# A forward substitution moved from VectorE to GpSimd in a hybrid decoder step, with the products that use it placed 29 pieces later

## The chip, the cores and the metric

The kernel runs on one NeuronCore of a Trainium2 chip, with five engines that run side by side: TensorE (PE in the profile), VectorE (DVE), ScalarE (ACT), GpSimd (POOL) and SyncE (SP), which here issues the DMA transfers. Each engine takes its instructions in the order in which they stand in its own queue; an instruction that waits for another engine holds up everything behind it on its own. The metric is the device time of one launch in microseconds. Of several runs the median counts.

## The reference

One inference step of a two-layer decoder for a prompt of 256 tokens, with 16 learned tokens ahead of it, and for 8 samples of one token. The sizes are D = 2048, width E = 4096 and 64 heads of 64. Layer 0 is RWKV-7 time mixing:

```python
def rwkv7_step(S, inp):
    r, d, k, v, kk, b = inp
    sa = jnp.einsum('bhij,bhj->bhi', S, kk)
    S = S * d[:, :, None, :] - sa[..., None] * b[:, :, None, :] + v[..., None] * k[:, :, None, :]
    return S, jnp.einsum('bhij,bhj->bhi', S, r)
...
    rkvz = jnp.einsum('btpd,pde->btpe', xm[:, :, :4], w_rkvz)
...
    S_fin, y = lax.scan(rwkv7_step, S0.astype(f32), ...)
    mean = jnp.mean(y, axis=-1, keepdims=True)
    var = jnp.mean(jnp.square(y - mean), axis=-1, keepdims=True)
    y = (y - mean) * lax.rsqrt(var + GN_EPS) * gn_g + gn_b
    y = y + jnp.sum(r_h * k_h * r_k, axis=-1, keepdims=True) * v_h
    y = y.reshape(B, T, WIDTH).astype(dt) * jax.nn.silu(z)
    return y @ w_out, S_fin.astype(S0.dtype), xn[:, -1]
```

Layer 1 is sliding-window attention. All is in float32. The change is in layer 0, in how the scan over the prompt's 272 tokens is computed.

## The kernel before

**Products.** Every weight matrix is read in tiles of 128 x 512 and split in two halves that TensorE multiplies fast: ACT casts the high half (`whi`, L195), DVE subtracts it from the tile to get the low half (`wlo`, L197), and PE makes three products for each pair (L218 to L220). High and low halves have five buffers each, so DVE can be at most five ahead of PE, and less while ACT waits for a buffer. A **piece** is six such products; a half serves two pieces.

**The mixing stage.** From about 130 to 1276 us PE works through the projections r, k, v, z and the first part of the output projection, piece by piece (`products`, L709). Between pieces it does the work of the scan. `drive` (L610) merges the streams: each stream is a Python generator, and `yield 5` means that its next part stands five pieces later in PE's order. So PE's order is written by hand. DVE, ACT and POOL have no written order: a scheduler places each of their instructions in its engine's queue when the program is built, and the queue is fixed from then on.

**The scan in chunks.** The tokens are taken in chunks of 64. Within a chunk the recurrence becomes a triangular system, which needs the inverse of a unit triangular 64 x 64 matrix for each head and chunk. Two units (four heads) are treated together; there are eight such **windows**, o = 0 to 7. In each:

- `scores` (L984) makes the matrices on PE, and ends with two sets of transposes of the keys (L1049, `ps_bk`).
- `substitute` (L1053) inverts the 16 x 16 diagonal blocks. POOL masks the blocks into N (L1064 to L1067), DVE transposes them to NL so that rows lie along the free dimension (L1069), and then come 14 steps, each a product into a scratch tile (L1075) and a sum into NL (L1077) that needs it, with 28 to 112 elements a partition. Two fills set the diagonal (L1079). DVE transposes the result twice, to TN (L1081) and TR (L1082), and ACT spreads TR into TT (L1085).
- `solve` (L1089) makes the 64 x 64 inverse of the blocks with small products on PE, the first of which read TN (L1102, `ps_so`). They stand 24 pieces (27 from o = 5 on) behind the last key transposes.
- `chain` (L1155) carries the state through the five chunks with this inverse.
- `group_norm` (L1256) normalises the window's result, turns it on PE in four turns (L1275, `ps_yt`) and evacuates each with one DVE instruction (L1276). Turns one and two share one pair of PSUM banks, turns three and four the next pair, and the pool has one pair: the third turn waits for the first two evacuations. These turns stand 36 pieces behind their chain, which is within the next window's substitution.

`prep` (L858) prepares the next units meanwhile. Six of its small copies for the samples (L932, `sm`) are on POOL.

Of the kernel before, what the change touches and what calls it, by code (L numbers as in the profile page):

```python
# [109 lines left out]
class Kernel:  # L110
# [942 lines left out]
    def substitute(self, o):  # L1053

        nc, rp = self.nc, self.rp
        V, A, G = nc.vector, nc.scalar, nc.gpsimd
        MU, AD = ALU.mult, ALU.add
        ND, N16, Noff = self.ND, self.N16, self.Noff
        w = lambda n, *s: rp.tile([128, *s], F32, tag=n, name=f"{n}{o}")
        ev = lambda n, *s: rp.tile([128, 512], F32, tag="ev", bufs=2, name=f"{n}{o}")[:, :s[0] * s[1]].rearrange(  # L1060
            "p (i t) -> p i t", t=s[1])
        mask = lambda i, n: self.cst(C_M16 + 16 * i, 16).unsqueeze(1).to_broadcast((128, n, 16))
        t1, t2 = ev("nd1", 20, 16), ev("nd2", 20, 16)
        G.tensor_tensor(t1, ND[:, :, 0:16], mask(0, 20), op=MU)  # L1064
        G.tensor_tensor(t2, ND[:, :, 16:32], mask(1, 20), op=MU)
        G.tensor_tensor(N16[:, 0:20], t1, t2, op=AD)
        G.tensor_tensor(Noff[:, :, 16:32], ND[:, 0:16, 16:32], mask(2, 16), op=MU)  # L1067
        NL = w("NL", 512)
        V.transpose(NL, N16.rearrange("p i t -> p t i"))  # L1069
        nl = NL.rearrange("p (t a s) -> p t a s", a=2, s=16)  # L1070
        for s in range(1, 15):
            n = 15 - s
            tmp = rp.tile([128, 112], F32, tag="stmp", name=f"stmp{o}_{s}")
            tv = tmp[:, :n * 2 * s].rearrange("p (t a j) -> p t a j", a=2, j=s)
            V.tensor_tensor(tv, nl[:, s + 1:16, :, s:s + 1].to_broadcast((128, n, 2, s)),  # L1075
                            nl[:, s:s + 1, :, 0:s].to_broadcast((128, n, 2, s)), op=MU)
            V.tensor_tensor(nl[:, s + 1:16, :, 0:s], nl[:, s + 1:16, :, 0:s], tv, op=AD)  # L1077
        for a in range(2):
            V.memset(NL[:, 16 * a:512:33], 1.0)  # L1079
        TN, TR = w("TN", 16, 32), w("TR", 16, 32)  # L1080
        V.transpose(TN.rearrange("p s i -> p (s i)"), nl.rearrange("p t a s -> p s a t"))  # L1081
        V.transpose(TR.rearrange("p t i -> p (t i)"), NL)  # L1082
        TT = rp.tile([128, 20, 64], F32, tag="TT", name=f"TT{o}")
        for b in range(4):
            A.activation(TT[:, :, 16 * b:16 * b + 16], TR[:, :, 0:20].rearrange("p t i -> p i t"), AF.Copy,  # L1085
                         scale=self.cst(C_M64 + 16 * b, 1))
        self.TT, self.TN, self.TR = TT, TN, TR

    def solve(self, o):  # L1089

        nc, rp = self.nc, self.rp
        V, A, G = nc.vector, nc.scalar, nc.gpsimd
        Noff, TT, TN, TR = self.Noff, self.TT, self.TN, self.TR
        ev = lambda n, *s: rp.tile([128, 512], F32, tag="ev", bufs=2, name=f"{n}{o}")[:, :s[0] * s[1]].rearrange(
            "p (i t) -> p i t", t=s[1])

        yield 24 if o < 5 else 27
        ps = self.bank(self.pe, f"ps_so{o}")
        Q = [slice(32 * q, 32 * q + 32) for q in range(4)]
        for i in range(16):  # L1100
            for q in Q:
                nc.tensor.matmul(ps[q, 16 * i:16 * i + 16], Noff[q, i], TN[q, :, i], start=True, stop=True)  # L1102
        ET = ev("ET", 16, 16)
        V.tensor_copy(ET, ps[:, 0:256].rearrange("p (i s) -> p i s", s=16))
        yield 4
        for i in range(16):
            for q in range(4):
                nc.tensor.matmul(ps[32 * q:32 * q + 16, 256 + 16 * i:272 + 16 * i], ET[Q[q], i], TR[Q[q], :, i],
                                 start=True, stop=True)
        for q in range(4):  # L1110
            r, c = slice(32 * q, 32 * q + 16), 16 + 32 * (q % 2)
            (A.copy if q % 2 else V.tensor_copy)(TT[r, 0:16, c:c + 16],
                                                 ps[r, 256:512].rearrange("p (i t) -> p i t", t=16))
        TN2 = ev("TN2", 16, 32)
        V.transpose(TN2.rearrange("p i s -> p (i s)"), TT[:, 0:16, 0:32])
        yield 7
        ps = self.bank(self.pe, f"ps_so2{o}").rearrange("p (i s) -> p i s", s=32)
        for i in range(16):
            for q in range(2):
                nc.tensor.matmul(ps[Q[2 * q + 1], i], self.N12[Q[2 * q], i], TN2[Q[2 * q], i], start=True, stop=True)  # L1120
        ET = ev("ET2", 16, 32)
        for q in range(2):
            r = Q[2 * q + 1]
            (A.copy if q else V.tensor_copy)(ET[r], ps[r])
        yield 5
        for i in range(16):
            for q in range(2):
                r = Q[2 * q + 1]
                nc.tensor.matmul(ps[Q[2 * q], i], ET[r, i], TT[r, i, 32:64], start=True, stop=True)
        for q in range(2):  # L1130
            r = Q[2 * q]
            (A.copy if q else V.tensor_copy)(TT[r, 0:16, 32:64], ps[r])
# [840 lines left out]
```

## Time and profile before

| what | value |
|---|---|
| median of 3 runs | 2118.64 us (2115.4 to 2123.16) |
| the profiled execution | 2118.32 us |
| its span, first to last instruction | 2116.5 us |
| TensorE's granted clock | 0.990 of full speed |
| PE busy | 2064.9 us, 98% |
| DVE busy | 1697.8 us, 80%, 4112 instructions |
| ACT busy | 1263.8 us, 60% |
| POOL busy | 122.5 us, 6%, 188 instructions |

A row of a group of instructions names line, engine, operation, the tile written and the tiles read, the shapes, how often, the busy time in us and the mean of one in ns, and then the idle time of the engine just before them and what ended it. A row of the order of time begins with the start and the duration in us. A row of the waits names who waited for whom, us in total, times and the longest. Products of PE overlap, so their starts tell the rate, not their durations.

### The profile page before, as it was taken

The page shows a single profiled execution, that of the slowest core. Times are in us where ns is not written, and L with a number is a line of the kernel's source. Part 1 is how long each engine was busy: PE and PEld are TensorE (multiplying, and loading weights), DVE is VectorE, ACT ScalarE, POOL GpSimd, SP SyncE. Part 2 cuts the span into 40 slices and gives each one's busy share as a digit, 9 for nine tenths or more (in the row PEclk, how much of TensorE's full clock was granted, in tenths as well). Part 3 has the DMA queues.
Part 4 walks back from the last instruction along what each step waited for, and adds up shares of the span by engine and source line. Part 5 has one row for each costly group of instructions (what it writes and reads, how often), then busy time and mean ns, then how long its engine had stood idle before and what let it go on. Part 6 is the DMA issues. An engine that isn't in the chain of part 4 may idle for free.

```text
span 2116.5 us, 55871 instructions
## 1 busy us (share of the span) xinstructions
PE 2064.9 (98%) x21420; PEld 1965.8 (93%) x21420; DVE 1697.8 (80%) x4112; ACT 1263.8 (60%) x2790; POOL 122.5 (6%) x188
## 2 busy tenths in 40 slices
PE   9999999899999999999999999999999999999997
PEld 7999899889899989899999999999999999999997
DVE  8867777687678878888888788997888888878885
ACT  3457766576766757767676445565565655544443
POOL 0011100001010010100100001100000000000000
PEclk9999999999999999999999999999999999999999
DMA  7898667658756876777657687757455444567774
GB/s 258 314 312 250 189 213 241 188 181 290 216 180 205 260 229 198 211 217 222 203 152 246 207 257 243 247 172 227 132 167 156 146 155 130 181 210 247 232 219 132
DMA packets 276356, 446.28 MB, mean 211 GB/s; under 512 B 54056, under 2 KB 97768, under 8 KB 275696
## 3 DMA queue, kind: packets, MB, share of 16 engines
q1 hardware_dynamic: 275656, 441.66, 66.6%
q8 instruction: 168, 2.75, 0.5%
q10 hardware_dynamic: 432, 1.05, 0.1%
q14 instruction: 100, 0.82, 0.1%
HBM read 381.69 MB, written 65.03 MB: 211 GB/s over the span
## 4 chain that ended last, share of the span: by engine, by line
PE 87%; DVE 5%; ACT 3%; DMA 3%; issue 2%; SPq 0%; POOL 0%; DVEq 0%; POOLq 0%; ACTq 0%
PE ps_z L218 6%; PE ps_z L219 6%; PE ps_z L220 6%; PE ps_k L218 3%; PE ps_ob L218 3%; PE ps_ob L220 3%; PE ps_v L218 3%; PE ps_ob L219 3%; PE ps_r L218 3%; PE ps_q L218 3%; PE ps_q L220 3%; PE ps_q L219 3%; PE ps_k L219 3%; PE ps_k L220 3%; PE ps_v L220 3%; PE ps_v L219 3%
## 5 line engine op out<-in xcount | busy, mean ns | idle before, releaser
L218 PE MATMUL ps_z<-mhlm,whi_z 128*128 128x280 f32 x512 | 158.6, 310 | 2.8 <-ACT sr L937 2.0
L219 PE MATMUL ps_z<-mhlm,whi_z 128*128 128x280 f32 x512 | 150.6, 294 | 0.0
L220 PE MATMUL ps_z<-mhlm,wlo_z 128*128 128x280 f32 x512 | 150.3, 294 | 0.0
L218 PE MATMUL ps_q<-bmh,whi_qb 128*128 128x264 f32 x512 | 150.0, 293 | 0.1
L218 PE MATMUL ps_z<-bmh,whi_zb 128*128 128x264 f32 x512 | 147.4, 288 | 0.0
L220 PE MATMUL ps_q<-bmh,wlo_qb 128*128 128x264 f32 x512 | 145.6, 284 | 0.6 <-DVE wlo_qb L197 0.6
L219 PE MATMUL ps_q<-bml,whi_qb 128*128 128x264 f32 x512 | 145.6, 284 | 0.0
L219 PE MATMUL ps_z<-bml,whi_zb 128*128 128x264 f32 x512 | 145.5, 284 | 0.0
L220 PE MATMUL ps_z<-bmh,wlo_zb 128*128 128x264 f32 x512 | 145.4, 284 | 0.0
L218 PE MATMUL ps_ob<-ghi,whi_ob 128*128 128x264 f32 x512 | 145.3, 285 | 0.0
L220 PE MATMUL ps_ob<-ghi,wlo_ob 128*128 128x264 f32 x512 | 144.6, 284 | 0.0
L219 PE MATMUL ps_ob<-glo,whi_ob 128*128 128x264 f32 x512 | 144.6, 283 | 0.0
L195 ACT CAST whi_ob<-raw_ob 128x512 fp32r<-128x512 f32 x128 | 79.1, 620 | 96.9 <-PE ps_ob L219 77.8
L195 ACT CAST whi_oa<-raw_oa 128x512 fp32r<-128x512 f32 x128 | 79.2, 620 | 88.0 <-PE ps_oa L219 30.6
L197 DVE TENSOR_TENSOR wlo_r<-raw_r,whi_r 128x512 fp32r<-128x512 f32 x128 | 87.8, 691 | 42.6 <-ACT whi_r L195 41.3
L218 PE MATMUL ps_v<-mhlm,whi_v 128*128 128x280 f32 x384 | 119.8, 312 | 0.4 <-ACT st L790 0.4
L218 PE MATMUL ps_k<-mhlm,whi_k 128*128 128x280 f32 x384 | 119.1, 310 | 1.0 <-ACT st L790 1.0
L195 ACT CAST whi_v<-raw_v 128x512 fp32r<-128x512 f32 x128 | 79.0, 619 | 65.8 <-PE ps_v L219 37.7
L197 DVE TENSOR_TENSOR wlo_v<-raw_v,whi_v 128x512 fp32r<-128x512 f32 x128 | 87.3, 687 | 36.9 <-ACT whi_v L195 35.6
L195 ACT CAST whi_zb<-raw_zb 128x512 fp32r<-128x512 f32 x128 | 78.2, 619 | 62.9 <-PE ps_z L219 38.5
L220 PE MATMUL ps_k<-mhlm,wlo_k 128*128 128x280 f32 x384 | 112.4, 293 | 2.1 <-issue 2.1
L219 PE MATMUL ps_v<-mhlm,whi_v 128*128 128x280 f32 x384 | 112.7, 293 | 0.0
(478 smaller groups left out, 7604.1 us busy)
## 6 DMA issues: line engine op xcount, KB each, us to landing
raw_k<-a_w_rkvz SPq DMA_DIRECT2D x128, 256.0 KB
raw_v<-a_w_rkvz SPq DMA_DIRECT2D x128, 256.0 KB
raw_r<-a_w_rkvz SPq DMA_DIRECT2D x128, 256.0 KB
raw_z<-a_w_rkvz SPq DMA_DIRECT2D x128, 256.0 KB
raw_oa<-a_w_out SPq DMA_DIRECT2D x128, 256.0 KB
raw_qb<-b_w_qz SPq DMA_DIRECT2D x128, 256.0 KB
raw_zb<-b_w_qz SPq DMA_DIRECT2D x128, 256.0 KB
raw_ob<-b_w_o SPq DMA_DIRECT2D x128, 256.0 KB
```

The costliest lines, as they stand in the source:

```text
L195: self.nc.scalar.copy(hi, src)
L197: return self.nc.vector.tensor_tensor(lo, src, hi.bitcast(F32), op=ALU.subtract)
L218: mm(ps, wh, xh, start=start, stop=False)
L219: mm(ps, wh, xl, start=False, stop=False)
L220: return mm(ps, wl, xh, start=False, stop=stop)
```

## The change

The 14 steps of the substitution and the two fills of the diagonal are issued on GpSimd instead of VectorE, in all eight windows. The three transposes stay on VectorE. The solve's first products stand 29 pieces behind the last key transposes in every window, instead of 24 (windows 0 to 4) and 27 (windows 5 to 7). Nothing is computed differently.

```diff
@@ substitute @@
         for s in range(1, 15):
             n = 15 - s
             tmp = rp.tile([128, 112], F32, tag="stmp", name=f"stmp{o}_{s}")
             tv = tmp[:, :n * 2 * s].rearrange("p (t a j) -> p t a j", a=2, j=s)
-            V.tensor_tensor(tv, nl[:, s + 1:16, :, s:s + 1].to_broadcast((128, n, 2, s)),
+            G.tensor_tensor(tv, nl[:, s + 1:16, :, s:s + 1].to_broadcast((128, n, 2, s)),
                             nl[:, s:s + 1, :, 0:s].to_broadcast((128, n, 2, s)), op=MU)
-            V.tensor_tensor(nl[:, s + 1:16, :, 0:s], nl[:, s + 1:16, :, 0:s], tv, op=AD)
+            G.tensor_tensor(nl[:, s + 1:16, :, 0:s], nl[:, s + 1:16, :, 0:s], tv, op=AD)
         for a in range(2):
-            V.memset(NL[:, 16 * a:512:33], 1.0)
+            G.memset(NL[:, 16 * a:512:33], 1.0)
@@ solve @@
-        yield 24 if o < 5 else 27
+        yield 29
         ps = self.bank(self.pe, f"ps_so{o}")
```

The scheduler places DVE's and POOL's instructions anew. In window 3 the stretch of DVE's queue around TN and TR reads, before:

```order
L197 TENSOR_TENSOR wlo_r_4_9909<-raw_r_4_9906,whi_r_4_9908 128x512
L1077 TENSOR_TENSOR NL_9548<-NL_9548,stmp_13_9586 128x4x13
L1276 SCALAR_TENSOR_TENSOR vT_5616<-ps_yt_0_9866,par,vT_5616 128x272
L1075 TENSOR_TENSOR stmp_14_9589<-NL_9548 128x28
L1077 TENSOR_TENSOR NL_9548<-NL_9548,stmp_14_9589 128x2x14
L197 TENSOR_TENSOR wlo_r_6_9915<-raw_r_6_9912,whi_r_6_9914 128x512
L1081 STREAM_TRANSPOSE TN_9594<-NL_9548 128x512
L1082 STREAM_TRANSPOSE TR_9595<-NL_9548 128x512
L1276 SCALAR_TENSOR_TENSOR vT_5616<-ps_yt_0_9866,par,vT_5616 128x272
L197 TENSOR_TENSOR wlo_r_8_9950<-raw_r_8_9947,whi_r_8_9949 128x512
L1276 SCALAR_TENSOR_TENSOR vT_6617<-ps_yt_2_9936,par,vT_6617 128x272
```

and with the change:

```order
L197 TENSOR_TENSOR wlo_r_4_9899<-raw_r_4_9896,whi_r_4_9898 128x512
L197 TENSOR_TENSOR wlo_r_6_9905<-raw_r_6_9902,whi_r_6_9904 128x512
L197 TENSOR_TENSOR wlo_r_8_9940<-raw_r_8_9937,whi_r_8_9939 128x512
L1081 STREAM_TRANSPOSE TN_9648<-NL_9602 128x512
L1082 STREAM_TRANSPOSE TR_9649<-NL_9602 128x512
L197 TENSOR_TENSOR wlo_r_10_9963<-raw_r_10_9960,whi_r_10_9962 128x512
L1276 SCALAR_TENSOR_TENSOR vT_5607<-ps_yt_0_9926,par,vT_5607 128x272
L197 TENSOR_TENSOR wlo_r_12_9981<-raw_r_12_9978,whi_r_12_9980 128x512
L1276 SCALAR_TENSOR_TENSOR vT_5607<-ps_yt_0_9926,par,vT_5607 128x272
L197 TENSOR_TENSOR wlo_r_14_10004<-raw_r_14_10001,whi_r_14_10003 128x512
L197 TENSOR_TENSOR wlo_r_0_10027<-raw_r_0_10024,whi_r_0_10026 128x512
L1276 SCALAR_TENSOR_TENSOR vT_6607<-ps_yt_2_9990,par,vT_6607 128x272
```

The steps of the substitution are gone from between the low halves, and both of the first two evacuations (L1276, `vT` from `ps_yt_0`) now stand behind TN, where one stood ahead of it. Between NL's transpose and TN this queue now has one product (L906) and eight low halves.

POOL's queue in the same window, from the masks on, with the change; before, the copies `sm` of L932 followed the masks directly:

```order
L1066 TENSOR_TENSOR N_1741<-nd_9596,nd_9597 128x320
L932 COPY sm_10038<-kT_9684 128x2x8
L1075 TENSOR_TENSOR stmp_1_9604<-NL_9602 128x28
L1077 TENSOR_TENSOR NL_9602<-NL_9602,stmp_1_9604 128x28
L932 COPY sm_10038<-ta_9422 128x2x8
L1075 TENSOR_TENSOR stmp_2_9607<-NL_9602 128x52
L1077 TENSOR_TENSOR NL_9602<-NL_9602,stmp_2_9607 128x26x2
```

The remaining steps follow one another without anything between them but the two fills. In windows 1 and 2 further `sm` copies stand among the steps.

PE's queue in window 3 around the solve's first products, before:

```order
L220 MATMUL ps_r_1_9905<-mhlm_23_2_8572,wlo_r_4_9909 128x280
L1102 MATMUL ps_so_9965<-TN_9594,Noff 32x16 x64
L1275 MATMUL ps_yt_2_9936<-consts,Y 128x128 x3
L218 MATMUL ps_r_0_9904<-mhlm_23_3_8634,whi_r_6_9914 128x280
L219 MATMUL ps_r_0_9904<-mhlm_23_3_8634,whi_r_6_9914 128x280
```

and with the change:

```order
L219 MATMUL ps_r_0_10073<-mhlm_23_0_8404,whi_r_0_10026 128x280
L220 MATMUL ps_r_0_10073<-mhlm_23_0_8404,wlo_r_0_10027 128x280
L1102 MATMUL ps_so_10093<-TN_9648,Noff 32x16 x64
L218 MATMUL ps_r_1_10074<-mhlm_23_0_8404,whi_r_0_10026 128x280
L219 MATMUL ps_r_1_10074<-mhlm_23_0_8404,whi_r_0_10026 128x280
```

Before, they stood between the third and the fourth turn of the group norm (L1275); now they stand five pieces behind the fourth.

## The prediction, made before the change was timed

> **What bounds the kernel now.** I read the page's busy shares first, then the waits of TensorE (PE), then the groups of VectorE (DVE) by line, then GpSimd's (POOL) prices, and last the order of time in two of the eight windows.
>
> From the page, share of the span:
>
> ```profile
> PE 2064.9 (98%) x21420; PEld 1965.8 (93%) x21420; DVE 1697.8 (80%) x4112; ACT 1263.8 (60%) x2790; POOL 122.5 (6%) x188
> ```
>
> PE is busy for 98% of the span and its order is written by hand, so the time changes only by what PE waits for. DVE at 80% is no bound by itself; POOL is nearly idle. PE's waits (us in total, times, longest) that name DVE inside the mixing stage:
>
> ```profile
> PE ps_yt L1275 <- DVE vT L1276: 8.0, 2, 6.9
> PE ps_so L1102 <- DVE TN L1081: 6.1, 2, 3.5
> ...
> PE ps_bo L954 <- DVE vT L955: 1.5, 2, 1.3
> ...
> PE ps_ch L1191 <- DVE X L1227: 1.1, 1, 1.1
> ```
>
> The second row is the substitution being late for the solve's first products: 6.1 us, in two windows of eight. The other six have room. So the most that the edit can win directly is 6.1 us, and all that DVE makes PE wait here is 16.7 us.
>
> **What is taken off DVE.** The groups of DVE by line, from 160 to 1260 us:
>
> ```profile
> L1077 DVE TENSOR_TENSOR NL<-NL,stmp 128x28 f32<-128x28 f32 (+6 forms) x112 | 26.9, 240 | 1.8
> ...
> L1075 DVE TENSOR_TENSOR stmp<-NL 128x28 f32<-128x28 f32 (+6 forms) x112 | 26.6, 238 | 1.6
> ```
>
> 224 small operations, 53.5 us in eight windows: 6.7 us of DVE work in each. DVE isn't the bound, so this is worth what PE waits for it, not 53.5 us.
>
> **What POOL needs for the same.** POOL's two-input operations by line, ns min/median/max:
>
> ```profile
> L1067 POOL TENSOR_TENSOR Noff<-F,consts x8: 737/747/3049, 225.7 to 1135.1; 128x256 f32<-128x256 f32 x8
> ...
> L1065 POOL TENSOR_TENSOR nd<-F,consts x8: 863/989/1335, 228.5 to 1137.1; 128x320 f32<-128x320 f32 x8
> ...
> L1450 POOL TENSOR_TENSOR sqacc<-sqacc,sqa x14: 791/1050/1117, 1291.5 to 1376.0; 128x280 f32<-128x280 f32 x14
> ```
>
> By the fastest of each, 256 elements take 737 ns and 320 take 863: 1.97 ns an element and 233 ns fixed (280 elements: 784, the row has 791). The substitution's products have 28, 52, 72, 88, 100, 108, 112 elements and back down to 28, 1120 in all, and the sums as many. So 28 x 0.233 + 2240 x 0.00197 = 10.9 us undisturbed. Every step needs the one before. The gap between dependent POOL operations, and the small copies that the change's order puts between the steps:
>
> ```profile
> 625.49 0.88 POOL L1065 TENSOR_TENSOR nd<-F,consts 128x320 f32<-128x320 f32 x1
> 626.44 1.21 POOL L1066 TENSOR_TENSOR N<-nd,nd 128x320 f32<-128x320 f32 x1
> 628.02 0.65 POOL L932 COPY sm<-kT 128x16 f32<-128x16 f32 x1 [0.37 <-DVE kT L904]
> 628.67 0.20 POOL L932 COPY sm<-ta 128x16 f32<-128x16 f32 x1
> ```
>
> 0.07 us lies between the first two (625.49 + 0.88 to 626.44): 28 x 0.07 = 2.0 us. Two copies at 0.2 us make 0.4. Sum: 13.3 us with nothing in the way.
>
> **Something is in the way.** The same stretch of window o=4 on both engines:
>
> ```profile
> 742.34 3.05 POOL L1067 TENSOR_TENSOR Noff<-F,consts 128x256 f32<-128x256 f32 x1 [5.81 <-ACT F L1023]
> ...
> 746.93 0.86 POOL L1065 TENSOR_TENSOR nd<-F,consts 128x320 f32<-128x320 f32 x1
> ```
>
> ```profile
> 745.41 0.67 DVE L197 TENSOR_TENSOR wlo_k<-raw_k,whi_k 128x512 fp32r<-128x512 f32 x1
> ...
> 747.15 1.20 DVE L197 TENSOR_TENSOR wlo_k<-raw_k,whi_k 128x512 fp32r<-128x512 f32 x1 [0.44 <-ACT whi_k L195]
> ```
>
> A DVE subtract that takes 0.67 us alone takes 1.20 beside a POOL operation; a POOL operation that takes 0.74 alone took 3.05 beside a run of DVE operations. [...] So the work moved to POOL does not run beside DVE's subtracts for nothing. Between the window's two transposes the changed order has eight low halves and one more two-input product on DVE. What one costs POOL is bounded below by nothing (it falls into POOL's gaps) and above by its whole 0.67 us. I take 0.4, between L1065's median and its slowest against its fastest (0.13 and 0.47) and nearer the latter, since POOL now always has a step waiting. 9 x 0.4 = 3.6: **the chain takes 16.9 us**, between 13.3 and 19.3.
>
> **What is behind it.** The order of the change puts DVE's transposes TN and TR in one place, behind eight low halves, and DVE stands at TN until POOL is through; before, 28 short operations stood there, each ready when its turn came. Behind TN wait a low half, the evacuation of the turned group norm (L1276), another low half and the second evacuation. PE's third turn (L1275) can't start before those two evacuations, since its two banks are single. How long PE takes to get there, in windows 3 and 4 (NL's transpose, TN, the evacuations; PE's third turn):
>
> ```profile
> 628.53 1.07 DVE L1069 STREAM_TRANSPOSE NL<-N 128x512 f32<-128x512 f32 x1
> ...
> 642.50 1.14 DVE L1081 STREAM_TRANSPOSE TN<-NL 128x512 f32<-128x512 f32 x1
> 643.57 0.67 DVE L1082 STREAM_TRANSPOSE TR<-NL 128x512 f32<-128x512 f32 x1
> 644.16 0.46 DVE L1276 SCALAR_TENSOR_TENSOR vT<-ps_yt,par,vT 128x272 f32<-128x272 f32 x1
> 644.54 0.67 DVE L197 TENSOR_TENSOR wlo_r<-raw_r,whi_r 128x512 fp32r<-128x512 f32 x1
> 645.25 0.50 DVE L1276 SCALAR_TENSOR_TENSOR vT<-ps_yt,par,vT 128x272 f32<-128x272 f32 x1
> ```
>
> ```profile
> 644.46 0.29 PE L219 MATMUL ps_r<-mhlm,whi_r 128*128 128x280 f32 x1
> 644.59 0.29 PE L220 MATMUL ps_r<-mhlm,wlo_r 128*128 128x280 f32 x1
> 644.72 0.50 PE L1275 MATMUL ps_yt<-consts,Y 128*128 128x128 f32 x3
> ```
>
> ```profile
> 749.27 1.08 DVE L1069 STREAM_TRANSPOSE NL<-N 128x512 f32<-128x512 f32 x1 [0.92 <-POOL N L1066]
> ```
>
> ```profile
> 768.40 0.38 PE L1275 MATMUL ps_yt<-consts,Y 128*128 128x128 f32 x2
> ```
>
> From NL's end to that turn PE takes 644.72 - 629.60 = 15.1 us and 768.40 - 750.35 = 18.1 us, 16.6 on average. From TN's start to the end of the second evacuation DVE takes 1.66 (642.50 to 644.16) + 0.71 + 0.38 + 0.71 + 0.50 = 4.0 us. So a chain of up to 12.6 us costs nothing, and one of 16.9 makes **PE wait 4.3 us**. This holds in windows 2, 3, 4, 6 and 7: 21.5 us. It comes earlier than the solve's first products, which the 29 pieces move away; they no longer are what is late.
>
> In windows 0 and 5 no evacuation stands behind TN, and the products' low halves are late instead. A low half serves 12 products 0.13 us apart (644.46, 644.59), 1.54 us. There are five buffers, so DVE is at most four ahead, 6.2 us, less the cast and the subtract that refill one:
>
> ```profile
> L195 ACT CAST whi_v<-raw_v 128x512 fp32r<-128x512 f32 x128 | 79.0, 619 | 65.8 <-PE ps_v L219 37.7
> ```
>
> 6.2 - 0.62 - 0.67 = 4.9 us. DVE gets to TN after some 8 x 1.54 = 12.3 us; with 13 two-input operations the chain is 13.3 + 13 x 0.4 = 18.5, DVE stands 6.2, and the next low half comes 6.2 + 1.7 + 0.7 = 8.6 us after the last, where PE wants it after 4.9 + 1.5 = 6.4: about 2.2. Window 0 has eight more such operations ahead of TN; 3 us each, 6 us. In window 1 DVE waits at the same place for a DMA in both kernels; I put 1 us.
>
> **Twenty-nine pieces.** A piece is six products, 0.77 us. The solve moves by 5 pieces five times and by 2 three times: the chain ends 31 x 0.77 = 24 us later in PE's order. PE does other products meanwhile, which costs nothing as long as there are some. Last window:
>
> ```profile
> 1258.39 0.55 PE L1275 MATMUL ps_yt<-consts,Y 128*128 128x128 f32 x3
> ```
>
> ```profile
> 1265.03 1.31 DVE L197 TENSOR_TENSOR glo<-gy,ghi 128x1120 fp32r<-128x1120 f32 x1
> ```
>
> The last turn's result is ready as an operand 1266.34 - 1258.39 = 8.0 us later. The changed order puts 72 products, 9.2 us, between that turn and the operand's first use. I put 0; without this cover it would be up to 8.
>
> **Sum.** 21.5 + 6 + 1 - 6.1 (the waits at L1102 go) = +22.4. The profiled execution took 2118.32 us, 1.8 more than its span and 0.3 under the median: **2141 us**. With a chain of 13.3 us: 5 x 0.7 - 6.1 = -2.6, 2116. With 19.3: 5 x 6.7 + 2 x 6 + 3 - 6.1 = +42, 2161.
>
> The nearest rows for the per-element price have inner rows of 16 elements or more; the substitution's have 1 to 14, with 64 bytes between them. [...]
>
> **The rivals.** *Short rows are dear.* If an element costs 1.55 times as much there (as L1065's slowest row to its fastest), 4.4 x 0.55 = 2.4 us come on top, the chain is 19.3 and the time 2161. For it: nothing in the trace has such rows. Against: L932's 16 elements take 0.20 us. [...]
>
> *The chain fits.* If DVE's two-input work falls into POOL's gaps, the chain is 13.3 to 14.5 us and PE waits 0.7 to 2 us a window: 2116 to 2124, no change that can be measured (0.5%, 10.6 us, is about what a measurement of this kernel can tell). For it: between L1065's median and its fastest lies only 0.13 us. Against: 3.05 for 0.74.
>
> *Faster.* DVE is rid of 6.7 us just where it is fullest. If the chain stays under 12.6 us everywhere, no wait at TN is passed on, and all 16.7 us that DVE makes PE wait could go: 2102. It decides at 12.6 us, under the 13.3 that POOL needs undisturbed; so only a lower fixed price than 233 ns would do it.
>
> **Chances.** The forecast 0.54, dear short rows 0.15, the chain fits 0.24, faster 0.07. The forecast's own range is 2128 to 2156; the range for 8 in 10 reaches down into the case that fits and up past the dear rows: 2112 to 2166. Faster by over 0.5% (under 2108): 0.07; within: 0.25; slower (over 2129): 0.68.
>
> **What would show it.** PE's wait for L1276 at L1275 grows from 8 us to 20 or more, in six or seven windows, and the wait for TN at L1102 is gone. DVE's waits get a row of TN waiting for POOL's NL, 4 to 7 us in each window. POOL's busy time about doubles, and L197 rows beside it take over 1 us. I am wrong in the price if L1075 and L1077 on POOL average far from 0.39 us plus 0.13 of blocking, and in the mechanism if TN starts late and PE doesn't wait, or if PE waits at L1102 still.

## The result: 2169.6 us, 2.4% slower

The changed kernel takes 2169.6 us (median of 4 runs, 2168.12 to 2171.73) against 2118.36 us in the same session: a ratio of 1.024, 95% interval 1.0221 to 1.0259. The prediction said 2141 us, 2112 to 2166: slower it is, but by 51 us and not by 22.

The page of the changed kernel, busy time by engine:

```profile
PE 2081.4 (96%) x21420; PEld 1977.7 (91%) x21420; DVE 1670.5 (77%) x3872; ACT 1263.7 (58%) x2790; POOL 217.9 (10%) x428
```

The span is 2166.3 us, 49.8 more than before. It splits in two. The time in which PE is not busy (span less busy) went from 51.6 to 84.9 us, **33.3 more**. And PE is busy for 2081.4 us where it was 2064.9, **16.5 more, with the same 21420 products**. The prediction spoke of the first part only.

The waits of the changed kernel (us in total, times, longest):

```profile
ACT TT L1085 <- DVE TR L1082: 40.1, 8, 5.8
DVE TN L1081 <- POOL NL L1077: 36.0, 8, 5.7
PE ps_yt L1275 <- DVE vT L1276: 25.3, 6, 5.4
PE ps_z L218 <- ACT st L790: 7.0, 1, 7.0
PE ps_so L1108 <- issue: 5.5, 4, 2.0
```

DVE stands at TN in all eight windows, 4.5 us on average, and ACT at its copies TT for 5.0 (36.0 and 40.1 us in eight windows): ACT too takes its instructions in order, and behind TT stand its casts and the evacuations of PE's results (L790). PE waits for what stands behind the two. Window 3 on DVE:

```profile
642.90 1.08 DVE L1069 STREAM_TRANSPOSE NL<-N 128x512 f32<-128x512 f32 x1
...
653.15 0.69 DVE L197 TENSOR_TENSOR wlo_r<-raw_r,whi_r 128x512 fp32r<-128x512 f32 x1 [0.65 <-ACT whi_r L195]
659.51 1.04 DVE L1081 STREAM_TRANSPOSE TN<-NL 128x512 f32<-128x512 f32 x1 [5.66 <-POOL NL L1077]
660.47 0.67 DVE L1082 STREAM_TRANSPOSE TR<-NL 128x512 f32<-128x512 f32 x1
661.06 0.65 DVE L197 TENSOR_TENSOR wlo_r<-raw_r,whi_r 128x512 fp32r<-128x512 f32 x1
661.63 0.49 DVE L1276 SCALAR_TENSOR_TENSOR vT<-ps_yt,par,vT 128x272 f32<-128x272 f32 x1
```

The eight low halves are done at 653.84, the chain at 659.5; TN starts at once, and the first evacuation ends at 662.12. PE in the same stretch:

```profile
657.13 0.29 PE L219 MATMUL ps_r<-mhlm,whi_r 128*128 128x280 f32 x1
657.26 0.29 PE L220 MATMUL ps_r<-mhlm,wlo_r 128*128 128x280 f32 x1
662.18 0.90 PE L1275 MATMUL ps_yt<-consts,Y 128*128 128x128 f32 x3 [4.63 <-DVE vT L1276]
662.73 0.58 PE L218 MATMUL ps_r<-mhlm,whi_r 128*128 128x280 f32 x1
663.11 0.43 PE L219 MATMUL ps_r<-mhlm,whi_r 128*128 128x280 f32 x1
663.35 0.43 PE L220 MATMUL ps_r<-mhlm,wlo_r 128*128 128x280 f32 x1
```

Ahead of the wait two products start 0.13 us apart; behind it 0.24 (663.11 to 663.35). Here is where PE's extra busy time lies. The same stretch in windows (length, PE busy, PEld, DVE, ACT, POOL, then PE's granted clock, DMA share, GB/s):

```profile
657.00:660.00 3.00, 0.55 (x5) 0.32 (x3) 0.49 (x1) 0.00 (x0) 2.08 (x9) 1.00 0.01 2
660.00:662.00 2.00, 0.00 (x0) 0.00 (x0) 2.00 (x4) 0.83 (x2) 0.00 (x0) 0.54 0.00 0
662.00:664.00 2.00, 1.82 (x8) 1.82 (x9) 1.22 (x3) 2.00 (x4) 0.00 (x0) 0.50 0.38 136
664.00:667.00 3.00, 3.00 (x15) 3.00 (x14) 1.31 (x2) 1.40 (x3) 0.00 (x0) 0.50 0.72 193
667.00:670.00 3.00, 3.00 (x27) 3.00 (x25) 1.26 (x3) 0.85 (x2) 0.00 (x0) 1.00 0.74 238
```

Some 2.6 us after PE has fallen idle (657.55 to about 660.2) its clock goes to half, and it stays there for 6.8 us, 4.8 us of them behind the wait's end. In three microseconds PE starts 15 products at half clock, and 27 in the next three. Over the mixing stage, before and then with the change:

```profile
160.00:1310.00 1150.00, 1116.23 (x13866) 1051.25 (x13866) 914.83 (x2053) 758.89 (x1671) 87.58 (x139) 0.99 0.70 218
```

```profile
160.00:1360.00 1200.00, 1133.84 (x13867) 1064.77 (x13866) 887.11 (x1813) 758.43 (x1672) 182.95 (x379) 0.97 0.67 209
```

The same 13867 products take 17.6 us more, at a granted clock of 0.97 instead of 0.99. Summed over short windows PE spent 34.1 us at half clock before its last product in the kernel before and 68.3 with the change. At a granted clock of 0.50 half of the added 34.2 us, 17.1, is what such time costs by estimate if PE has work throughout; measured are 16.5.

### The profile page after: what moved, and what is told of

Same layout as the page of the kernel before. It is cut to its first block, busy times and chain, and to the rows that moved or that the text cites. A ratio compares the mean times of both kernels' runs of the same rounds, so it can differ in the third digit from the quotient of the medians.

```text
span 2166.3 us, 55895 instructions
## 1 busy us (share of the span) xinstructions
PE 2081.4 (96%) x21420; PEld 1977.7 (91%) x21420; DVE 1670.5 (77%) x3872; ACT 1263.7 (58%) x2790; POOL 217.9 (10%) x428
## 3 DMA queue, kind: packets, MB, share of 16 engines
q8 instruction: 168, 2.75, 0.5%
## 5 line engine op out<-in xcount | busy, mean ns | idle before, releaser
L195 ACT CAST whi_oa<-raw_oa 128x512 fp32r<-128x512 f32 x128 | 79.2, 621 | 87.8 <-PE ps_o L219 34.2
L218 PE MATMUL ps_v<-mhlm,whi_v 128*128 128x280 f32 x384 | 121.2, 316 | 3.0 <-ACT st L790 2.0
L197 DVE TENSOR_TENSOR wlo_r<-raw_r,whi_r 128x512 fp32r<-128x512 f32 x128 | 89.0, 702 | 41.2 <-ACT whi_r L195 39.4
L197 DVE TENSOR_TENSOR wlo_k<-raw_k,whi_k 128x512 fp32r<-128x512 f32 x112 | 77.9, 701 | 55.3 <-ACT whi_k L195 55.1
L197 DVE TENSOR_TENSOR wlo_v<-raw_v,whi_v 128x512 fp32r<-128x512 f32 x128 | 87.8, 691 | 41.5 <-ACT whi_v L195 39.9
L195 ACT CAST whi_zb<-raw_zb 128x512 fp32r<-128x512 f32 x128 | 78.2, 619 | 62.6 <-PE ps_z L219 38.5
L220 PE MATMUL ps_v<-mhlm,wlo_v 128*128 128x280 f32 x384 | 114.1, 297 | 0.0
```

The source lines that it names most:

```text
L195: self.nc.scalar.copy(hi, src)
L197: return self.nc.vector.tensor_tensor(lo, src, hi.bitcast(F32), op=ALU.subtract)
L218: mm(ps, wh, xh, start=start, stop=False)
L220: return mm(ps, wl, xh, start=False, stop=stop)
```

## The experiments

Three theories. **Theory 1**: DVE and ACT stand in order behind GpSimd's chain, and PE's clock halves after each long wait. **Theory 2**: GpSimd and DVE slow each other down. **Theory 3**: the later solve has a price. All twelve kernels, with the two of the case; "not busy" is the span less PE's busy time, "half clock" is summed as above.

| kernel | median us | ratio to before, 95% interval | PE not busy | PE busy | half clock |
|---|---|---|---|---|---|
| before | 2118.36 | 1 | 51.6 | 2064.9 | 34.1 |
| the change | 2169.60 | 1.0240 (1.0221 to 1.0259) | 84.9 | 2081.4 | 68.3 |
| pieces29 | 2127.49 | 1.0048 (1.0032 to 1.0065) | 59.1 | 2066.7 | 27.3 |
| pool_old | 2151.01 | 1.0162 (1.0144 to 1.0180) | 78.2 | 2076.6 | 54.6 |
| late_tn | 2127.19 | 1.0041 (1.0022 to 1.0060) | 61.6 | 2063.8 | 20.5 |
| busy_turn | 2191.93 | 1.0353 (1.0337 to 1.0368) | 83.1 | 2105.7 | 58.0 |
| busy_second | 2167.10 | 1.0226 (1.0207 to 1.0245) | 67.8 | 2096.7 | 30.7 |
| half_chain | 2153.02 | 1.0154 (1.0135 to 1.0173) | 73.5 | 2079.9 | 54.6 |
| late_old | 2128.25 | 1.0041 (1.0026 to 1.0056) | 59.7 | 2069.2 | 41.0 |
| spread29 | 2124.96 | 1.0024 (1.0012 to 1.0035) | 53.6 | 2069.9 | 37.5 |
| act_late | 2165.34 | 1.0231 (1.0216 to 1.0246) | 89.2 | 2079.4 | 64.9 |
| spread_dve | 2117.68 | 0.9997 (0.9981 to 1.0012) | 47.8 | 2062.5 | 20.5 |
| spread_pool | 2118.95 | 1.0004 (0.9992 to 1.0015) | 51.5 | 2062.2 | 17.1 |
| idle_copy | 2144.92 | 1.0131 (1.0106 to 1.0157) | 71.4 | 2071.3 | 47.8 |

Twelve of these kernels have the same 21420 products (all but the two busy ones). Over them PE's busy time rises with its time at half clock, by 0.39 us for each, with a correlation of 0.97.

The three last columns are those of one profiled execution, whose span can lie some us beside the median (spread_dve: 2110.3, at the lower end of its runs).

### The two halves of the change, one at a time

pieces29 is before with the second edit alone, pool_old the change without it:

```diff
# pieces29: against before
-        yield 24 if o < 5 else 27
+        yield 29
# pool_old: against the changed kernel
-        yield 29
+        yield 24 if o < 5 else 27
```

> Only the 29 pieces; the substitution stays on DVE. Theory 1 (DVE and ACT stand in order behind GpSimd's chain, and PE's clock halves after each long wait): nothing of the loss is in the pieces. The 6.1 us of PE's wait for TN at L1102 go and nothing else changes: 2110 to 2122 us, ratio 0.997 to 1.002. Theory 3 (the solve, 24 us later in PE's order, makes what follows it late; the 16 us of new PE waits at L1191, L218 and L1108 are its price): about 2118 + 16 = 2134 us, ratio 1.008, with these waits in the trace.

> Only the substitution on GpSimd; the pieces stay at 24 and 27. Theory 1: the loss is here: 2162 to 2175 us (after: 2169.6), with about 25 us of PE's wait at L1275 and 60 to 75 us at half clock. Theory 3: without the later solve 16 us less than after, about 2153 us.

Neither theory had it whole: pieces29 lies between their numbers, and pool_old even below theory 3's. The 29 pieces cost 10 us by themselves (0.48%), GpSimd's substitution 34 us (1.62%), and the two together some 7 us more than the sum, hardly more than the three intervals leave open. In pool_old the stand is the one of the change, 37.5 us of DVE at TN and 30.8 of PE at L1275, and PE spends 54.6 us at half clock.

What the 29 pieces cost is on the page of pieces29's waits:

```profile
PE ps_so L1108 <- issue: 10.9, 7, 3.3
PE ps_ch L1191 <- ACT X L1227: 3.8, 3, 2.6
PE ps_yt L1275 <- DVE vT L1276: 2.9, 3, 2.3
...
PE ps_ch L1191 <- DVE X L1227: 2.3, 2, 1.4
```

The waits for TN and for the evacuations are as good as gone, as predicted, and in their place PE stands at the solve's second group of products, for nothing that the profile names. A smaller part is theory 3's: in the chain that follows the solve PE waits 6.1 us at L1191, where before has 1.3. Window 3 on PE:

```profile
658.20 1.27 PE L1102 MATMUL ps_so<-TN,Noff 32*32 32x16 f32 x128
662.85 1.23 PE L1108 MATMUL ps_so<-TR,ET 32*16 32x16 f32 x126
667.33 0.21 PE L1108 MATMUL ps_so<-TR,ET 32*16 32x16 f32 x2 [3.25 <-issue]
```

PE runs 126 of 128 products, stands for 3.25 us and then runs the last two, which need nothing that the 126 did not have. In the list of DMA queues over the whole of before stands a row of instructions, and between 664.5 and 666 us of pieces29 one packet of it:

```profile
q8 instruction: 168, 2.75, 0.5%
```

```profile
q8 instruction: 1, 0.02, 3.9%
```

2.75 MB in 168 packets are 16 KB each, and 2 x 21420 products and weight loads in 168 packets are 255 instructions each: this is PE's own program, fetched in blocks. (With the semaphore instructions PE has 43021 records in before, 256 for each packet.) Each of the solve's two groups is 256 instructions in 1.2 us, a block's worth, where elsewhere in the mixing stage one block lasts about 10 us. The packet lands at 665.8 and PE goes on at 667.3. All fourteen traces bear it out. PE stands 70 times for over 0.3 us without a named cause. Counted along PE's records, 68 of these stands fall on the same place in a block of 256, number 193 or 194, and in each of the 68 a packet of this queue lands 1.2 to 1.8 us before PE goes on.

### Is it the clock?

Unused products ahead of a waiting turn take away PE's idleness and no wait. busy_turn has them ahead of the third turn, busy_second ahead of the second:

```diff
+                self.cur = ps[0] if h < 7 else None        # in `products`
 ...
+            for _ in range(18 if j == 2 and self.cur is not None else 0):   # busy_second: j == 1
+                nc.tensor.matmul(self.cur[:, 384:512], self.ident, self.ident, start=False, stop=False)
             for c in range(3):
                 nc.tensor.transpose(ps[:, 128 * c:128 * c + 128], ...
```

> After, with 18 products of 128 x 128 (some 3.8 us, their results are read by nobody) ahead of the third turn L1275 in every window but window 5: PE works where it waited. Theory 1 (a wait of PE is followed by half clock): PE waits 1 us instead of 4 to 5, the half clock behind these turns (41 of the 68 us) goes, and although no work is removed the kernel is up to 41/2 = 20 us faster: 2150 to 2160 us. Rival (the clock has no part; PE's products are slower for another reason): the products fill the wait and change nothing, 2168 to 2173 us.

2191.9 us. The third turn was the wrong place, which corrected the picture: PE's 25 us at the turns stayed, and of the 30.2 us that the seven groups take 22 were simply added. The turn that waits is the second, for the first evacuation (661.63 + 0.49 against 662.18 in the rows above), though the two have a bank each.

> After, with the 18 unused products of 128 x 128 (4.2 us by their 18 in the last run) now ahead of the second turn L1275, which is the one that waits, in windows 2 to 7 (and once behind the last window). Theory 1 (a wait of PE is followed by half clock): PE's 25 us at L1275 fall to about 8 (window 1 has no products), the half clock behind these turns goes (68 us of half clock before, 35 or less now), and although no work is taken out the time falls by 10 to 17 us: 2152 to 2160 us. Rival (PE's products are slower for another reason, the clock follows it): the products fill the waits, 4 us are lost where nothing waits, 2170 to 2176 us.

2167.1 us: the gain did not come, PE's wait at the turns fell to 16.3 us and not to 8, and still the run tells what it was made for. Its page, and the time of the unused products alone:

```profile
PE 2096.7 (97%) x21672; PEld 1994.0 (92%) x21672; DVE 1670.2 (77%) x3872; ACT 1263.1 (58%) x2790; POOL 217.9 (10%) x428
```

```profile
0.00:2165.00 2165.00, 29.26 (x252) 28.80 (x252) 0.99 0.66 206
```

The unused products take 29.3 us. Without them PE is busy for 2096.7 - 29.3 = 2067.4 us, 14 less than in the change and within 2.5 us of before, and its time at half clock is 30.7 us instead of 68.3. So with the idleness the slow clock goes, and the products run at their old pace. That the time did not fall is arithmetic: 14 us of clock and 17.1 us of idleness were won, and 29.3 us of products paid for them.

Over eight of these traces (before, the change, pieces29, pool_old, late_tn, half_chain, act_late, idle_copy) PE waited 2.4 us or longer 52 times; 48 of these waits have a stretch of half clock beginning within 5.5 us of their start. Of 58 waits between 1.4 and 2.4 us, 26 have one. Over all fourteen traces it is 69 of 79 and 41 of 91. Before PE's last product the stretches last 3.4, 6.8, 10.2 or, once in spread29, 13.7 us. So a wait of 2.4 us sufficed in nearly all cases and one of 1.4 in some (the shortest, with no longer wait near it, is 1.43 us at L1102 in the change).

### Is it the standing or the company?

late_tn leaves GpSimd's chain and the 29 pieces as they are, and puts the two transposes behind four more low halves. `issue_after` queues what is in its block behind the named instruction of the same engine; `los` and `his` hold the low halves and the casts issued so far:

```diff
     def substitute(self, o):
 ...
-        TN, TR = w("TN", 16, 32), w("TR", 16, 32)
-        V.transpose(TN.rearrange("p s i -> p (s i)"), nl.rearrange("p t a s -> p s a t"))
-        V.transpose(TR.rearrange("p t i -> p (t i)"), NL)
-        TT = rp.tile([128, 20, 64], F32, tag="TT", name=f"TT{o}")
-        for b in range(4):
 ...
     def solve(self, o):
 ...
-        yield 29
+        yield 25
+        with self.tc.issue_after(self.los[-1].ins):
+            TN, TR = w("TN", 16, 32), w("TR", 16, 32)
+            V.transpose(TN.rearrange("p s i -> p (s i)"), nl.rearrange("p t a s -> p s a t"))
+            V.transpose(TR.rearrange("p t i -> p (t i)"), NL)
+        with self.tc.issue_after(self.his[-1].ins):
+            TT = rp.tile([128, 20, 64], F32, tag="TT", name=f"TT{o}")
+            for b in range(4):
 ...
+        yield 4
```

> After, with the two transposes TN and TR put on DVE behind four more low halves (12 instead of 8), behind the first turned group norm's two evacuations, and ACT's four copies TT likewise later; GpSimd's chain and the 29 pieces stay. Theory 1: nobody stands behind the chain any more. DVE's 36 us of waiting at TN and ACT's 40 us at TT fall below 8, PE's 25.3 us at L1275 and the 7.0 us in window 5 go, and with them the 17 us of slower clock: 2169.6 - 25.3 - 7.0 - 17 = 2120 us, 2105 to 2125. Theory 2 (GpSimd's work beside DVE's slows DVE, whatever stands where): 2150 us or more.

2127.2 us, above the 2105 to 2125 expected, since the 29 pieces have a price of their own; the time is that of pieces29 to 0.3 us. The waits of late_tn:

```profile
ACT TT L1100 <- DVE TR L1096: 9.8, 8, 2.3
PE ps_so L1114 <- issue: 6.5, 5, 2.5
DVE TN L1095 <- POOL NL L1077: 4.8, 4, 1.6
PE ps_yt L1281 <- DVE vT L1282: 4.0, 3, 2.3
```

DVE's stand falls from 36.0 to 4.8 us and ACT's from 40.1 to 9.8, and 42 us of the kernel's time go with them, although GpSimd does the same work beside DVE (230.7 us busy). Theory 2 as it was put, GpSimd's work slowing DVE, has nothing left in this change. The cost lies in where the scheduler put TN against the chain's end. Contention has a share in that all the same: the chain takes some 3.9 us more in each window beside DVE's operations than by its fastest steps (below), and DVE stands 4.5 us there. No run has this chain without DVE's operations beside it.

act_late frees ACT alone: TN and TR stay, only the four copies TT move as above.

> After, with ACT's four copies TT (L1085) put behind the casts of 25 pieces later, and DVE's TN and TR left where after has them: only ACT is freed from standing. If ACT's standing has its own price (window 5: 7.0 us of PE's wait for ACT's st, and its half clock of 10.2 us): ACT's 40 us of waiting for TR fall below 8, the 7.0 us go and 5 us of clock with them, 2158 us (2154 to 2163). If DVE's standing alone sets the time: 2167 to 2172 us.

2165.3 us, 4 less than the change, and the two intervals overlap. PE's 7.0 us in window 5 are gone, and of its other large waits none: that for the evacuations is 29.4 us, and DVE still stands 35.8 at TN. So freeing ACT alone is worth some 4 us, and nearly all of the 42 needs DVE freed. What ACT's standing would cost with DVE free no run shows.

half_chain asks how the price depends on the chain's length. It leaves out steps 8 to 14:

```diff
-        for s in range(1, 15):
+        for s in range(1, 8):
             n = 15 - s
```

> After, with the steps 8 to 14 of the substitution left out (half the elements, 14 of 28 operations), so that GpSimd's chain is about 8 us instead of 15.9. Theory 1 with the bound of the prediction (a chain of up to about 12 us costs nothing): all of the chain's price goes, what is left is that of the 29 pieces: 2127 us, 2122 to 2131. Rival (each us of the chain costs the same, by contention or in the chain of dependences): half of the price goes, about 2148 us.

2153.0 us: more than half of the price is left, and the bound of 12 us is refuted as such. The waits, and window 3 on DVE:

```profile
DVE TN L1081 <- POOL NL L1079: 29.0, 8, 4.2
```

```profile
642.77 0.76 DVE L197 TENSOR_TENSOR wlo_r<-raw_r,whi_r 128x512 fp32r<-128x512 f32 x1 [0.86 <-ACT whi_r L195]
646.88 1.09 DVE L1081 STREAM_TRANSPOSE TN<-NL 128x512 f32<-128x512 f32 x1 [3.36 <-POOL NL L1079]
```

The chain takes 8 us, and DVE still stands 3.6 us in each window, because TN now stands behind three to five low halves instead of seven or eight. With the chain the scheduler moved TN as well, as if it placed TN where it takes the chain to end, and too soon in both kernels. The rival's number (2148) is nearer, but not for the rival's reason.

idle_copy puts GpSimd's load beside before, unneeded by anybody:

```diff
+        X = ev("X", 2, 256)
+        xl = N16.rearrange("p (t a) s -> p t a s", a=2)
+        for s in range(1, 15):
+            ...
+            G.tensor_tensor(xv, xl[:, s + 1:16, :, s:s + 1]..., xl[:, s:s + 1, :, 0:s]..., op=MU)
+            G.tensor_tensor(xw, xl[:, s + 1:16, :, 0:s], xv, op=AD)
         for s in range(1, 15):
```

> Before (substitution on DVE, 24 and 27 pieces), and beside it GpSimd does 28 operations of the same shapes in each window whose results nobody reads: GpSimd's load of after without anybody waiting for it. Theory 1 (only standing in order costs): DVE's two-input operations lose at most 28 x 0.1 us in each window, off PE's path for the most part: 2114 to 2126 us. Theory 2 (contention of the two engines): the 34 us that pool_old lost come back here, 2140 us or more.

2144.9 us, against theory 1 as I had put it. DVE's two groups of the substitution, and the largest wait of PE:

```profile
L1083 DVE TENSOR_TENSOR stmp<-NL 128x28 f32<-128x28 f32 (+6 forms) x112 | 38.7, 345 | 1.5
L1085 DVE TENSOR_TENSOR NL<-NL,stmp 128x28 f32<-128x28 f32 (+6 forms) x112 | 38.2, 341 | 1.9
```

```profile
PE ps_yt L1283 <- DVE vT L1284: 25.3, 9, 8.5
```

Each short operation of DVE takes 343 ns instead of 239, 2.9 us in each window: the size that I had allowed. What I had wrong is that this is off PE's path. The evacuations stand between these operations, PE's wait for them goes from 8.0 to 25.3 us, and some 26 us are lost. The queues are not what changed: PE and ACT have the order of before, and DVE too, but for two pairs of neighbours among 4112, and nobody waits for the added work. Contention is real, then, where both engines run short two-input operations, as here. In the change DVE has none left there, and its large subtracts hardly suffer: in the mixing stage L197 takes 702 ns on average, against 693 before.

### Can the two edits be had without their price?

> The substitution on GpSimd, TN and TR behind two or three more low halves than in after (10 or 11), and the solve's first products at 24 and 27 pieces as before. If the prices of the two parts are separate, the 10 us of the 29 pieces go too and DVE's 53 us of short operations are gone: 2108 to 2118 us. If TN is then late for L1102 (chain 15.9 + transposes 2.2 + NL 1.1 against 24 x 0.77 = 18.5 us), PE waits up to 1 us in each window: 2118 to 2126 us.

late_old is late_tn with 21 pieces to TN and 24 and 27 to the first products. 2128.3 us: TN is not late for L1102, but at 21 pieces it is early for the chain again, and L1275 waits 12.9 us.

spread29 is pieces29 with `yield 8` for the `yield 4` between the solve's two groups; spread_dve and spread_pool keep 27 and 4 pieces in the last window:

```diff
-        yield 29
+        yield 29 if o < 7 else 27
 ...
-        yield 4
+        yield 8 if o < 7 else 4
         for i in range(16):
```

> Pieces29 (the substitution on DVE, 29 pieces) with the second group of products, L1108, 8 pieces behind the first, L1102, instead of 4. Theory A (PE's instructions come from memory in blocks of 16 KB, 256 instructions; the two groups of 128 products and weight loads 3.4 us apart use them faster than they come, so PE stands inside L1108 for 12.3 us in all): the wait inside L1108 falls below 4 us, 2127 - 8 = 2119 us, 2114 to 2122. Theory B (the solve's end comes too late for what follows): 4 pieces more make it worse, 2127 to 2133 us.

The waits of spread29:

```profile
PE ps_oa L218 <- ACT ghi L195: 4.0, 1, 4.0
PE ps_dy L1337 <- DVE dy L1334: 3.4, 1, 3.4
...
PE ps_so L1108 <- issue: 1.5, 2, 1.2
```

Both theories hold a part. Eight pieces apart, the two groups hardly run out of instructions any more: 10.9 us become 1.5. But the last window, with no next one behind which to hide, ends later, and two new waits of 7.4 us stand there.

> Spread29 (substitution on DVE, 29 pieces, L1108 8 pieces behind L1102), but with 27 and 4 pieces in the last window, whose end stood in the way: there PE waited 7.4 us for the last group norm and ran at half clock for 13.7 us. Theory A (the instruction stream sets the price of the 29 pieces): 2125 - 7.4 - 6.8 = 2111 us, 2107 to 2116, faster than before. Theory B (a later solve costs in every window): 2119 to 2125 us.

> Late_tn (substitution on GpSimd, nobody standing behind it) with the same two changes as spread_dve. Late_tn's 9.1 us of PE's wait in the second group of products go, by theory A: 2127 - 9 = 2118 us, 2111 to 2121. If GpSimd's work beside DVE's has a price of its own, spread_pool is slower than spread_dve by it; theory 1 says by 3 us or less, theory 2 (contention) by 10 or more.

2117.7 and 2119.0 us: the price of the 29 pieces is gone in both, and both take what before takes. The first lies 1.7 us above the range expected of it, the second within its own. The last window still costs spread_dve 5.6 us of PE's waits (3.0 at L1337, 2.6 at L1275) and 10.2 us at half clock. Between the two kernels lies 1.3 us, and their intervals overlap, so with nobody standing behind it GpSimd's substitution neither costs nor gains anything that these runs can tell, though it relieves DVE of 32 us (1703.0 to 1671.2 us busy). No version is measurably faster than the kernel before.

## Why the prediction was right and wrong, step by step

- **The waits at L1102 go (6.1 us).** Right: 1.4 us are left, and not for TN.
- **GpSimd's chain takes 16.9 us, 13.3 to 19.3.** Right: 15.9 us on average from first to last step, 15.0 to 17.3. The groups of the changed kernel:

```profile
L1075 POOL TENSOR_TENSOR stmp<-NL 128x28 f32<-128x28 f32 (+6 forms) x112 | 56.9, 508 | 19.1 <-DVE NL L1069 9.1 <-DVE rstk L298 2.5
L1077 POOL TENSOR_TENSOR NL<-NL,stmp 128x28 f32<-128x28 f32 (+6 forms) x112 | 51.6, 461 | 8.0
```

  By the fastest of each step's runs the steps need 9.7 us (predicted 10.9: 112 elements take 0.40 us, 28 take 0.24) and busy are 13.6: 3.9 us of blocking, where 3.6 were put. An element costs (402 - 235) / 84 = 2.0 ns, what it costs in long rows. Rows of one element cost a little more (a sum of 28 elements takes 258 ns in the first step, in rows of one, and 238 in the last, in rows of 14), but with 9.7 us in all the rival of dear short rows is out. That an operation of DVE costs GpSimd at most its whole 0.67 us, from which the 19.3 comes, no run shows; the longest chain in the change took 17.3. That L197 beside the chain would take over 1 us was wrong: in the mixing stage three do, and six did before. It is GpSimd that pays.
- **DVE stands at TN, and PE waits for the evacuations behind it, 4.3 us in each of five windows.** Right in kind and nearly in size: in those five windows (2, 3, 4, 6 and 7) PE waits 2.4, 4.6, 3.5, 5.4 and 4.1 us at L1275, 20.0 in all where 21.5 were put. The row of 25.3 us holds 5.25 us of window 1 besides, which before has too (6.9): there the wait became 1.7 shorter, where 1 us more was put. Wrong in detail: it is the second turn that waits for the first evacuation, not the third for both. And "up to 12.6 us costs nothing" is no property of the chain: half_chain, at 8 us, still cost 25.5 us more than pieces29. What counts is how far the queue's order is ahead of the chain. From NL's end to TN's start the substitution took 18.7 us on average on DVE, and takes 16.0 on GpSimd. It became *shorter*; before, each of its 28 short operations stood among the low halves and held them up little, and now one instruction holds up everything.
- **Windows 0 and 5 wait 3 us each for late low halves.** Wrong in kind, and in window 0 right in size: there an evacuation (L955) does stand behind TN, for which PE waits 2.25 us, and for a low half behind it 0.6. Window 5 waits 7.0 us for ACT's evacuation behind TT. That ACT stands in order as well was left out; act_late puts it at some 4 us.
- **Twenty-nine pieces: nothing.** This step failed: 10 us alone (pieces29), and the cover that the prediction named, other products, was there. What it missed is PE's own program: with two groups of 256 short instructions some 3.4 us apart PE stands 10.9 us in L1108, behind the landing of its packets, and 1.5 us with the groups eight pieces apart (spread29); spread_dve takes the 10 us away again (it also puts the last window back to 27 pieces). A smaller part are the waits at L1191, 6.1 us where before has 1.3. Why 24 pieces escape most of it is not separated: there the groups are 3.8 to 5.3 us apart in four windows, but in the other four no farther than at 29.
- **"The time changes only by what PE waits for."** This is the step that failed most. PE's products themselves became slower, by 16.5 of the 49.8 us, since the clock halved after long waits (68.3 us at half clock, 34.1 before). The page of before had it in sight: a mean granted clock of 0.990 with three waits over 2.4 us. In waits the prediction's sum was 22.4 us against 33.3 measured. By PE's rows the places that it named come to 21.1 us: +17.3 at L1275, 2.9 in window 0, 7.0 in window 5, -6.1 for TN at L1102. The other 12.2 us it put at nothing: 5.2 us of PE out of instructions at L1102 and L1108 and 5.1 us more at L1191, both of which pieces29 has too, and 1.9 us in small rows. How the prices of the two edits overlap stays open.

In the sum, then, the mechanism at TN was right and its term well sized. That the named places together come within 1.3 us of the forecast is in part luck, since window 5 waits 4 us more, by another engine, and windows 1 and 5 wait less at L1275. A second price of the same waits (clock, 16.5 us) and a second effect of the other edit (10 us alone) were put at zero.

## What to carry to other kernels

Work moved to another engine is paid for where its result is awaited: look at what the order puts behind the first instruction that needs it, on every engine that stands in order, and move that instruction back before judging the engine. Price a wait of PE over some 2.4 us at its length and half of what lies behind it of the 3.4 to 10 us at half clock (48 of 52 such waits had a stretch of it here). And count instructions, not only time, where hundreds of tiny products stand close together: here two groups of 256 instructions some 3.4 us apart left PE standing for up to 3.25 us.

## What was not expected of the hardware

- Half clock after waits as short as 1.4 to 2.4 us (26 of 58 in eight traces), and in nearly all from 2.4 us on (48 of 52), in stretches of 3.4, 6.8, 10.2 and 13.7 us.
- PE running dry of instructions inside a group of ready products, for up to 3.25 us, and in 68 of 70 such stands at the same place in its blocks of 256 instructions, 1.2 to 1.8 us behind the landing of a 16 KB packet in the instruction queue.
- GpSimd and DVE slow each other down one-sidedly: DVE's two-input operations of 28 to 112 elements go from 239 to 343 ns beside GpSimd's (idle_copy), those of 512 elements only from 693 to 702 (the change); there GpSimd's take 0.40 us alone and mostly 0.73 or more when they meet one (112 elements).
